# The low part of every fourth weight block made by an accumulating DMA instead of VectorE

## The chip, the cores and the metric

The kernel runs on one core of a Trainium2 chip. The metric is the device time of one execution, in microseconds. The core has five engines with instruction streams of their own: TensorE (PE in the profile, with its weight loads as PEld), VectorE (DVE), ScalarE (ACT), GpSimd (POOL) and SyncE (SP). Sixteen DMA engines move data; a transfer is issued from the stream of SP, ACT or POOL.

## The reference

Two transformer blocks run one after the other on 256 tokens of width 2048, all in float32. The first block has softmax attention with ALiBi (8 heads), a retention layer (4 heads), gates, and a gated feed-forward layer of inner width 5632. The second has gated linear attention, differential attention, and a feed-forward layer with a short convolution, again of inner width 5632. Cut to what matters here, the work is a chain of dense products with weights that are each used once:

```python
proj = h @ w_in                       # 2048 x 13312, first block
merged = sigmoid(ga) * (oa @ w_o_attn) + sigmoid(gr) * (orr @ w_o_ret)
x = x + merged @ w_out
g, u = split(rms_norm(x, g_ffn) @ w_ffn_in)       # 2048 x 11264
x = x + (silu(g) * u) @ w_ffn_out                 # 5632 x 2048
...                                   # second block, of the same kind
```

The weights come to some 500 MB in float32.

## The kernel before

Each matrix product in float32 is made of three products of reduced operands. A weight block `w` is split into a high part (`hi`, `w` rounded to the format fp32r) and a low part (`lo = w - hi`); the activations are split in the same way. TensorE then adds `x_hi*hi`, `x_lo*hi` and `x_hi*lo` in one accumulator (lines 1170 to 1172, and lines 1208 and 1210 for the products with the weights as the stationary operand).

The weights are cut into 946 blocks of 128 x 1024 float32 (512 KB). The class `Sched` streams them in one fixed order. Three of its methods matter here:

- `load` (line 79) issues the DMA of a block into a tile `wraw` from SP's stream. There are 4 such tiles (`RAW_BUFS`), so the load of block n+4 waits until everything that reads the tile of block n is done.
- `split` makes `hi` by a ScalarE copy (line 100, tile `whi`) and `lo` by a VectorE subtraction (line 101, tile `wlo`). There are 4 tiles of each (`PART_BUFS`), so the split of block n waits until TensorE has finished with block n-4. A few blocks of two tasks, whose numbers are in the set `roomy`, get a tile `wparts` of another pool.
- `take` is called ahead of the products of each block. It asks for loads up to 6 blocks ahead and for splits up to 3 blocks ahead (2 for the first 16 blocks), and hands out the parts of the next block.

The norms of line 356 on POOL divide the program into four stages: the first block's mixer (288 weight blocks), its feed-forward layer (264), the second block's mixer (130) and its feed-forward layer (264).

The rest of the work (attention, retention, gated linear attention, norms, evacuations of accumulators) is written as generators, which `tick` advances by a step after each block; so it stands between the blocks in each engine's stream. Every engine works through its stream in order. SP's stream holds little but the loads. POOL's stream holds 49 tensor operations and 10 loads of other inputs.

For a block that is used as the moving operand, TensorE runs 12 products of 512 columns: for two groups of 128 tokens and two groups of 128 inputs, one with `hi` and the high part of x, one with `hi` and the low part, one with `lo`.

Of the kernel before, what the change touches and what calls it, by code (L numbers as in the profile page):

```python
# [14 lines left out]
AF = mybir.ActivationFunctionType  # L15
ALU = mybir.AluOpType
# [28 lines left out]
class Sched:  # L45
# [39 lines left out]
    def split(self, upto):  # L85
        nc = self.nc
        if self.hold is not None:
            upto = min(upto, self.hold)
        while self.n_split <= min(upto, len(self.blocks) - 1):
            self.load(self.n_split)  # L90
            n = self.blocks[self.n_split].shape[1]
            raw = self.raw.pop(self.n_split)
            if self.n_split in self.roomy:
                both = self.room([P, 2, 1024], F32R, name="wparts")
                hi, lo = both[:, 0], both[:, 1]
            else:
                hi = self.wp.tile([P, 1024], F32R, name="whi", tag="whi", bufs=PART_BUFS)
                lo = self.wp.tile([P, 1024], F32R, name="wlo", tag="wlo", bufs=PART_BUFS)
            for c in self.cuts(self.n_split, n):
                nc.scalar.activation(hi[:, c], raw[:, c], AF.Copy)  # L100
                nc.vector.tensor_tensor(lo[:, c], raw[:, c], hi[:, c].bitcast(F32), op=ALU.subtract)  # L101
                if self.n_split == 0:
                    self.between()
            self.parts[self.n_split] = (hi, lo)
            self.n_split += 1
# [79 lines left out]
def body(ctx, tc, A, out):  # L185
# [62 lines left out]
    def halves(dst, src, scale=None):  # L248
        split(dst[:, 0], dst[:, 1], src, scale)
# [154 lines left out]
    def turned(key, f0, srcs, use=None, then=None, gain=None, wait=2):  # L404

        def part(j):
            def fn():
                m = mtile()
                turn(m, srcs, j)
                f = f0 + 2 * j  # L410
                if use is not None:
                    use(f, m)
                    return
                h_tile(key, f)
                dst = st[key][f // 4][:, f % 4:f % 4 + 2]
                if gain is None:
                    split(dst[:, :, 0], dst[:, :, 1], pairs(m))
                else:
                    highs_lows([(dst[:, i], m[:, cols(i, S)], gain(f + i)) for i in range(2)])
            return fn  # L420
        for j in range(2):
            step_of(key, f0 + 2 * j, part(j), wait + j)
            if then is not None:
                step_of(key, f0 + 2 * j, lambda f=f0 + 2 * j: then(f), wait + j + 1)
# [610 lines left out]
    def act_split(f):  # L1035
        h_tile("act", f)
        dst = st["act"][f // 4][:, f % 4:f % 4 + 2]
        split(dst[:, :, 0], dst[:, :, 1], pairs(st.pop(("cv", f))))
# [313 lines left out]
```

## Time and profile before

| what | value |
|---|---|
| median of 2 runs | 2761.0 us (2760.97 to 2761.03) |
| the profiled execution's own time | 2761.08 us |
| its span, first to last instruction | 2759.3 us |
| TensorE busy | 99% of the span |
| VectorE busy | 54% |
| ScalarE busy | 47% |
| GpSimd busy | 2% |
| the 16 DMA engines busy, SP's queue | 53.3% |
| granted TensorE clock, mean | 0.999 of full speed |

A row of a group of instructions reads: line, engine, operation, the tile written and the tiles read, shapes, count; then the busy time and the mean duration in nanoseconds; then the idle time of that engine just before them, and what ended it. A row of a timeline reads: start and duration in microseconds, engine, line, operation, tiles, count, and in brackets the idle time before it and what ended that.

### The profile page before, as it was taken

What the parts mean: (1) busy time and instruction counts of PE and PEld (TensorE: products, weight loads), DVE (VectorE), ACT (ScalarE), POOL (GpSimd) and SP (SyncE); (2) the same over time, 40 slices, a digit from 0 to 9 for tenths busy, and PEclk for the clock granted to TensorE, in tenths of its full rate; (3) what the DMA queues carried; (4) which work ended last, traced back from release to release, by engine and by line L of the source; (5) the groups of instructions that cost most, each with busy time, mean ns of one, the idle gap of its engine ahead of it and who ended that gap; (6) DMA issues with size and microseconds to landing.
All of it is one profiled execution on the core that took longest, in us unless ns stands there. A gap on an engine that the chain in (4) does not pass through costs nothing.

```text
span 2759.3 us, 33343 instructions
## 1 busy us (share of the span) xinstructions
PE 2728.7 (99%) x12876; PEld 2274.1 (82%) x12876; DVE 1502.6 (54%) x1732; ACT 1299.0 (47%) x1673; POOL 61.6 (2%) x63
## 2 busy tenths in 40 slices
PE   8999999999999999999999999999989999999998
PEld 6888788888888888888888888888878888888887
DVE  4456555554455554545455547775555554455555
ACT  5445444444444444334444454554455554445543
POOL 0000000000000000000000001110000000000000
PEclk9999999999999999999999999999999999999999
DMA  7554446555555555555555555445545555555554
GB/s 255 178 180 167 160 168 217 195 187 194 191 185 189 190 191 184 192 196 191 191 185 189 189 202 174 145 145 191 183 169 185 189 182 192 194 187 183 187 190 151
DMA packets 141936, 511.41 MB, mean 185 GB/s; under 512 B 16912, under 2 KB 17296, under 8 KB 141008
## 3 DMA queue, kind: packets, MB, share of 16 engines
q1 hardware_dynamic: 140256, 500.62, 53.3%
q0 software_dynamic: 1376, 8.65, 0.9%
q8 instruction: 101, 1.65, 0.2%
q14 instruction: 59, 0.48, 0.0%
q10 hardware_dynamic: 144, 0.01, 0.0%
HBM read 507.11 MB, written 2.10 MB: 185 GB/s over the span
## 4 chain that ended last, share of the span: by engine, by line
PE 97%; DVE 1%; ACT 1%; issue 0%; DMA 0%; SPq 0%; POOLq 0%; DVEq 0%; POOL 0%; ACTq 0%
PE acc L1172 27%; PE acc L1170 27%; PE acc L1171 27%; PE acc L1208 8%; PE acc L1210 4%; PE m L402 2%; PE m L797 1%; DMA wraw<-in_w_va 0%; DVE hx L239 0%; DVE wlo L101 0%; PE m L520 0%; PE m L599 0%; PE m L452 0%; DVE x L239 0%; ACT junk L336 0%
## 5 line engine op out<-in xcount | busy, mean ns | idle before, releaser
L101 DVE TENSOR_TENSOR wlo<-wraw,whi 128x1024 fp32r<-128x1024 f32 (+1 forms) x934 | 1144.4, 1226 | 1003.9 <-ACT whi L100 999.1
L100 ACT ACTIVATE whi<-wraw 128x1024 fp32r<-128x1024 f32 (+1 forms) x934 | 986.7, 1058 | 944.5 <-PE acc L1171 896.0
L1170 PE MATMUL acc<-whi,hx 128*128 128x512 f32 x2160 | 858.1, 397 | 11.3 <-ACT hx L230 5.9
L1172 PE MATMUL acc<-wlo,hx 128*128 128x512 f32 x2160 | 844.1, 391 | 0.5 <-DVE wlo L101 0.5
L1171 PE MATMUL acc<-whi,hx 128*128 128x512 f32 x2160 | 842.6, 390 | 0.0
L1170 PEld LDWEIGHTS acc<-whi,hx 128*128 128x128 f32 x2160 | 406.4, 188 | 94.7 <-ACT whi L100 6.3
L1172 PEld LDWEIGHTS acc<-wlo,hx 128*128 128x128 f32 x2160 | 406.1, 188 | 88.0 <-DVE wlo L101 1.7
L1171 PEld LDWEIGHTS acc<-whi,hx 128*128 128x128 f32 x2160 | 406.8, 188 | 83.6 <-issue 1.9
L1208 PE MATMUL acc<-hx,whi 128*128 128x512 f32 x912 | 330.6, 404 | 0.0
L1170 PE MATMUL acc<-whi,act 128*128 128x512 f32 (+1 forms) x704 | 271.0, 385 | 0.0
L1172 PE MATMUL acc<-wlo,act 128*128 128x512 f32 (+1 forms) x704 | 269.8, 383 | 0.0
L1171 PE MATMUL acc<-whi,act 128*128 128x512 f32 (+1 forms) x704 | 269.8, 383 | 0.0
L1210 PE MATMUL acc<-hx,wlo 128*128 128x256 f32 x912 | 255.7, 280 | 0.0
L1208 PEld LDWEIGHTS acc<-hx,whi 128*128 128x128 f32 x912 | 171.3, 188 | 38.9 <-issue 0.5
L1210 PEld LDWEIGHTS acc<-hx,wlo 128*128 128x128 f32 x912 | 172.4, 189 | 1.0 <-issue 0.5
L1172 PEld LDWEIGHTS acc<-wlo,act 128*128 128x128 f32 x704 | 132.3, 188 | 26.3
L1170 PEld LDWEIGHTS acc<-whi,act 128*128 128x128 f32 x704 | 132.4, 188 | 25.5
L1171 PEld LDWEIGHTS acc<-whi,act 128*128 128x128 f32 x704 | 132.4, 188 | 25.4
L228 ACT ACTIVATE t<-acc 128x256 f32<-128x256 f32 x57 | 21.9, 383 | 96.7 <-PE acc L1210 96.6
L239 DVE SCALAR_TENSOR_TENSOR cv<-m,c_conv_w,cv 128x255 f32<-128x255 f32 x88 | 40.4, 480 | 24.0 <-ACT cv L1018 22.5
L1170 PE MATMUL acc<-whi,mg 128*128 128x512 f32 x128 | 50.7, 396 | 0.0
L1172 PE MATMUL acc<-wlo,mg 128*128 128x512 f32 x128 | 49.9, 390 | 0.0
(279 smaller groups left out, 1825.4 us busy)
## 6 DMA issues: line engine op xcount, KB each, us to landing
wraw<-in_w_f SPq DMA_DIRECT2D x352, 512.0 KB, 3.4
wraw<-in_w_f1o SPq DMA_DIRECT2D x88, 512.0 KB, 4.3
wraw<-in_w_f2o SPq DMA_DIRECT2D x78, 512.0 KB, 3.3
wraw<-in_w_ga SPq DMA_DIRECT2D x34, 512.0 KB, 3.4
wraw<-in_w_vr SPq DMA_DIRECT2D x32, 512.0 KB, 3.3
wraw<-in_w_gr SPq DMA_DIRECT2D x32, 512.0 KB, 3.2
wraw<-in_w_gret SPq DMA_DIRECT2D x32, 512.0 KB, 3.3
wraw<-in_w_or SPq DMA_DIRECT2D x32, 512.0 KB, 3.4
```

The source lines that it names most:

```text
L100: nc.scalar.activation(hi[:, c], raw[:, c], AF.Copy)
L101: nc.vector.tensor_tensor(lo[:, c], raw[:, c], hi[:, c].bitcast(F32), op=ALU.subtract)
L228: nc.scalar.activation(out, in_, AF.Copy)
L239: nc.vector.scalar_tensor_tensor(out, a, s, b, op0=op0, op1=op1)
L402: nc.tensor.transpose(m[:, (i * len(srcs) + k) * P:][:, :P], src[:, (n * j + i) * P:][:, :P], ident)
L797: nc.tensor.matmul(m[:, ks], prev[1][:, ks], prev[0][:, ks], start=True, stop=True)
L1170: nc.tensor.matmul(accs[k], x[:, 0], hi[:, w], start=b, stop=False)
L1171: nc.tensor.matmul(accs[k], x[:, 1], hi[:, w], start=False, stop=False)
L1172: nc.tensor.matmul(accs[k], x[:, 0], lo[:, w], start=False, stop=e)
L1208: nc.tensor.matmul(acc, hi[:, w], x.rearrange("p a b -> p (a b)"), start=(k == first), stop=False, skip_group_check=True)
L1210: nc.tensor.matmul(acc[:, S:], lo[:, w], x[:, 0], start=False, stop=(k == last), skip_group_check=True)
```

## The change

For every block whose number has the remainder 3 by 4, from block 11 on and outside `roomy`, the low part is made in another way. ScalarE writes the high part as before, and then the same rounding with the sign turned over into `lo`, so `lo = -hi`. A DMA issued from POOL's stream then adds the raw block onto it: `lo = -hi + w`. VectorE's subtraction is left out for these blocks. Nothing else differs, and the numbers of tiles stay as they were. The program holds 231 such blocks: in POOL's stream 71 of these DMAs stand ahead of the norm that closes the first stage, 66 more ahead of the second, 31 ahead of the third, and 63 after that.

```diff
+            if self.n_split % 4 == 3 and self.n_split > 8 and self.n_split not in self.roomy:
+
+                nc.scalar.activation(hi[:, :n], raw[:, :n], AF.Copy)
+                nc.scalar.activation(lo[:, :n], raw[:, :n], AF.Copy, scale=-1.0)
+                nc.gpsimd.dma_start(lo[:, :n], raw[:, :n], accum_op=ALU.add)
+                self.parts[self.n_split] = (hi, lo)
+                self.n_split += 1
+                continue
             for c in self.cuts(self.n_split, n):
                 nc.scalar.activation(hi[:, c], raw[:, c], AF.Copy)
                 nc.vector.tensor_tensor(lo[:, c], raw[:, c], hi[:, c].bitcast(F32), op=ALU.subtract)
```

ScalarE's stream in the first feed-forward layer. Before, around the split of the activations (`act`), the copies of the high parts stand alone:

```order
335 L228 ACTIVATE act<-m 128x2x256
336 L100 ACTIVATE whi<-wraw 128x1024 x6
337 L637 ACTIVATE gate<-acc,r_x_97 128x512 x2
338 L100 ACTIVATE whi<-wraw 128x1024 x9
339 L228 ACTIVATE act<-m 128x2x256
```

With the change, the same place (the lines of the program are 8 further on):

```order
620 L108 ACTIVATE whi<-wraw 128x1024 x2
621 L101 ACTIVATE whi<-wraw 128x1024
622 L102 ACTIVATE wlo<-wraw 128x1024
623 L108 ACTIVATE whi<-wraw 128x1024 x3
624 L645 ACTIVATE gate<-acc,r_x_97 128x512 x2
```

After every three copies (line 108) there are two for one block (lines 101 and 102), the second into `wlo`.

SP's stream with what each load waits for, where the loads of the first feed-forward layer's output weights begin. Before, every load waits for VectorE, which is the subtraction that read the tile last:

```order
401 L79 DMA wraw<-in_w_f 128x1024 [waits DMAHW0_49,DVE_49]
402 L79 DMA wraw<-in_w_f1o 128x1024 [waits DMAHW1_49,DVE_49]
403 L79 DMA wraw<-in_w_f1o 128x1024 [waits DMAHW2_49,DVE_49]
404 L79 DMA wraw<-in_w_f1o 128x1024 [waits DMAHW3_49,DVE_49]
405 L79 DMA wraw<-in_w_f1o 128x1024 [waits DMAHW4_49,DVE_49]
406 L79 DMA wraw<-in_w_f1o 128x1024 [waits DMAHW5_49,DVE_49]
```

With the change:

```order
401 L79 DMA wraw<-in_w_f 128x1024 [waits DMAHW1_49,DVE_49]
402 L79 DMA wraw<-in_w_f1o 128x1024 [waits DMAHW0_49,DMASW1_49]
403 L79 DMA wraw<-in_w_f1o 128x1024 [waits DMAHW2_49,DVE_49]
404 L79 DMA wraw<-in_w_f1o 128x1024 [waits DMAHW3_49,DVE_49]
405 L79 DMA wraw<-in_w_f1o 128x1024 [waits DMAHW5_49,DVE_49]
406 L79 DMA wraw<-in_w_f1o 128x1024 [waits DMAHW4_49,DMASW2_49]
```

Every fourth load now waits for a DMA of POOL's queue (the semaphores DMASW) in place of VectorE, and the loads behind it in SP's stream come after it.

POOL's stream around the attention of the second block, with the change:

```order
167 L103 DMA wlo<-wraw 128x1024 [waits DMASW0_49,DMAHW4_49,PE_49,Activation_49]
168 L789 TENSOR_TENSOR Kl<-E,gqk 128x256 [waits DVE_49]
169 L789 TENSOR_TENSOR Kl<-E,gqk 128x256 x2
170 L103 DMA wlo<-wraw 128x1024 [waits DMASW2_49,DMASW1_49,DMAHW0_49,PE_49,Activation_49]
171 L789 TENSOR_TENSOR Kl<-E,gqk 128x256 [waits DVE_49]
```

Before, the operations of line 789 (then 781) stood there with no DMA between them. Now the accumulating DMAs (line 103), which wait for ScalarE, stand in the same stream.

## Rows read from the trace of the kernel before

**Rows 1.** The page: busy time of each engine; the chain of waits.
```profile
PE 2728.7 (99%) x12876; PEld 2274.1 (82%) x12876; DVE 1502.6 (54%) x1732; ACT 1299.0 (47%) x1673; POOL 61.6 (2%) x63
PE 97%; DVE 1%; ACT 1%; issue 0%; DMA 0%; SPq 0%; POOLq 0%; DVEq 0%; POOL 0%; ACTq 0%
```

**Rows 2.** The waits of TensorE: waited for, us in total, times, longest.
```profile
PE acc L1172 <- DVE wlo L101: 0.5, 1, 0.5
...
PEld acc L1172 <- DVE wlo L101: 1.7, 3, 0.9
```

**Rows 3.** The page's groups: the two halves of the split.
```profile
L101 DVE TENSOR_TENSOR wlo<-wraw,whi 128x1024 fp32r<-128x1024 f32 (+1 forms) x934 | 1144.4, 1226 | 1003.9 <-ACT whi L100 999.1
L100 ACT ACTIVATE whi<-wraw 128x1024 fp32r<-128x1024 f32 (+1 forms) x934 | 986.7, 1058 | 944.5 <-PE acc L1171 896.0
```

**Rows 4.** Timeline of ScalarE, first feed-forward layer.
```profile
1000.04 1.06 ACT L100 ACTIVATE whi<-wraw 128x1024 fp32r<-128x1024 f32 x1 [1.66 <-PE acc L1171]
1002.76 1.06 ACT L100 ACTIVATE whi<-wraw 128x1024 fp32r<-128x1024 f32 x1 [1.66 <-PE acc L1171]
1005.48 1.06 ACT L100 ACTIVATE whi<-wraw 128x1024 fp32r<-128x1024 f32 x1 [1.66 <-PE acc L1171]
1008.20 1.06 ACT L100 ACTIVATE whi<-wraw 128x1024 fp32r<-128x1024 f32 x1 [1.66 <-PE acc L1171]
1009.79 0.69 ACT L637 ACTIVATE gate<-acc,r_x 128x512 f32<-128x512 f32 x1 [0.53 <-PE acc L1172]
```

**Rows 5.** Timeline of all engines, the same stretch: VectorE and SP.
```profile
1001.13 1.23 DVE L101 TENSOR_TENSOR wlo<-wraw,whi 128x1024 fp32r<-128x1024 f32 x1 [1.49 <-ACT whi L100]
...
1002.39 13.93 SPq L79 DMA_DIRECT2D wraw<-in_w_f  x6
```

**Rows 6.** The tile wraw: time from issue to landing of its 947 loads.
```profile
DMA to landing us min/median/max: 3.0/3.6/11.0
```

**Rows 7.** DMA issues from POOL: count, KB each, median us from issue to landing.
```profile
xr<-in_x_rows POOLq DMA_DIRECT2D x2, 1024.0 KB, 8.9
x<-in_x_rows POOLq DMA_DIRECT2D x2, 1024.0 KB, 8.4
post<-in_attn_post_norm POOLq DMA_DIRECT2D x1, 1024.0 KB, 6.8
post<-in_ffn_post_norm POOLq DMA_DIRECT2D x1, 1024.0 KB, 8.5
decay<-in_decay POOLq DMA_DIRECT2D x1, 768.0 KB, 6.8
e<-in_mk POOLq DMA_DIRECT2D x1, 512.0 KB, 9.1
```

**Rows 8.** Timeline of POOL: the norms that close the four stages, one issue.
```profile
860.18 1.62 POOL L356 TENSOR_TENSOR r_x<-ms,neghalf 128x2 f32<-128x2 f32 x1 [402.45 <-DVE ms L355]
1592.86 1.61 POOL L356 TENSOR_TENSOR r_x<-ms,neghalf 128x2 f32<-128x2 f32 x1 [731.06 <-DVE ms L355]
...
1895.26 0.62 POOL L955 DMA_DIRECT2D post<-in_attn_post_norm  x1
2025.80 1.64 POOL L356 TENSOR_TENSOR r_x<-ms,neghalf 128x2 f32<-128x2 f32 x1 [24.72 <-DVE ms L355]
2745.06 0.66 POOL L356 TENSOR_TENSOR r_f<-ms,neghalf 128x1 f32<-128x1 f32 x1 [716.47 <-DVE ms L355]
```

**Rows 9.** Windows: engines' busy time, granted clock, DMA share, GB/s.
```profile
860.00:1593.00 733.00, 733.00 (x3291) 606.69 (x3290) 371.83 (x344) 317.05 (x341) 1.76 (x2) 1.00 0.56 190
...
2005.00:2010.00 5.00, 4.21 (x15) 3.05 (x15) 4.06 (x7) 2.79 (x9) 0.00 (x0) 0.71 0.46 144
```

**Rows 10.** Timeline of TensorE around the turn of the second block.
```profile
1999.73 0.39 PE L1172 MATMUL acc<-wlo,hx 128*128 128x512 f32 x1
2003.42 0.63 PE L402 MATMUL m<-c_ident,x 128*128 128x128 f32 x4 [3.31 <-DVE x L239]
...
2017.61 0.66 PE L402 MATMUL m<-c_ident,x 128*128 128x128 f32 x4 [1.66 <-DVE x L239]
2018.02 0.48 PE L1170 MATMUL acc<-whi,hx 128*128 128x512 f32 x1
```

## The prediction

> **What bounds the kernel now.** I read the busy times and the chain of waits first. TensorE is busy for 99% of the span and makes up 97% of the chain [rows 1]; the reader is to see that nothing but its stream of products sets the end. Then its waits: for the low parts that VectorE makes it waits 0.5 + 1.7 = 2.2 us in the whole run [rows 2]. So taking work from VectorE can give back about 2 us at most. The question is only whether the new way of making the low part is late.
>
> For that I read how early a block is ready, in a stretch of pure weight products. ScalarE starts a copy at 1000.04, 1002.76, 1005.48 and 1008.20 us, each time let go by TensorE's last use of a high part [rows 4]. So a block takes 2.72 us, four take 10.88 us, and a split starts as soon as the parts of four blocks earlier are free. Since three other blocks come in between, the low part has 3 x 2.72 us, and two products of its own block (0.45 us), before it is missed: 8.6 us. Now it takes 1.06 us on ScalarE, and VectorE ends at 1001.13 + 1.23 = 1002.36, which is 2.3 us after the start [rows 4, 5]. SP's next load is issued at 1002.39, at once after it [rows 5]: the raw tile is what that load waited for. A load lands 3.6 us after its issue in the median, 3.0 at least [rows 6]. From the start of a split to the landing of the load that takes over its raw tile is thus 2.3 + 3.6 = 5.9 us, and 10.88 us are there: 5.0 us to spare.
>
> **What the change removes.** 231 subtractions of 1.23 us, 283 us of VectorE [rows 3]. They lie beside TensorE's work, so this is worth at most the 2.2 us above; I take nothing.
>
> **What it adds on ScalarE.** 231 second copies of 1.06 us, 245 us [rows 3]. ScalarE is idle for 1.66 us ahead of each copy [rows 4], so the second fits and leaves 0.6 us. An evacuation of 0.69 us [rows 4] that falls right there is late by some tenths, and the accumulators have spare tiles; I take nothing, with 0.1 us as an upper end in the round trip below, which is inside its uncertainty. In POOL's stream the Kl operations of the second mixer now stand behind a DMA that waits for ScalarE. Their results are used a step of the generator, one block, later: nothing from below, 31 DMAs x 2.2 us = 68 us from above. I take nothing, since that stage also has the longest time for a block.
>
> **What it adds in DMA time: two round trips.** Call D the time from ScalarE's second copy to the landing of the accumulating DMA. After the copies (2 x 1.06 us and two handovers, 2.2 us) come D and then the use. The first round trip is that of the part tiles: D may be 8.6 - 2.3 = 6.3 us before TensorE waits. The second is that of the raw tiles, and it is tighter: every fourth load now waits for the accumulating DMA, and four blocks later its block is split. One turn takes 2.3 + D + 3.6 us. It fits in 10.9 us up to D = 5.0 us. Above that TensorE waits for the rest once in four blocks, and the turn itself is then the pace.
>
> D has no row, since nothing accumulates before. From below: a plain load of 512 KB from SP lands after 3.0 us at the fastest [rows 6]. From above: the slowest POOL load, 512 KB behind two others, takes 9.1 us [rows 7]. The transfer reads 512 KB of raw block and 512 KB of negated high part, so each DMA engine takes in as much as for a plain 1 MB; the nearest rows are the loads of 1 MB from POOL that had the queue to themselves, 6.8 and 8.5 us [rows 7]. I take the lower, 6.8 us, because here the weight loads partly wait for this DMA instead of running beside it, and nothing of it comes from outside the core's own memory. POOL's stream is held for 0.6 us by an issue [rows 8], which is inside the 6.8.
>
> Against this stands a rule. These rows say 6.8 us or more for 1 MB. The Trainium skill, "DMA: Bandwidth & Descriptors", section "Anatomy of one DMA — SWDGE (gpsimd) path", fits a transfer issued from GpSimd by 2.0 us plus the bytes over 436 GB/s; an estimate from that page is 3.2 us for 512 KB and 4.4 us for 1 MB. By it the turn is 2.3 + 4.4 + 3.6 = 10.3 us and the sum is nothing; by the row it is the sum below. The row has the weight loads beside it, as here (in such a stage the engines are busy 56% of the time [rows 9]), so I go by the row. The skill's "Collectives: The Full Stack", on why a reduce-scatter moves half of what an all-gather does, says that an add in a DMA takes two source reads on one ring, which is the doubling used here; no run before shows it.
>
> **The sum.** The turn is 2.3 + 6.8 + 3.6 = 12.7 us. What four blocks take differs by stage, because other products lie between them. The norms that close the stages start at 860.2, 1592.9, 2025.8 and 2745.1 us [rows 8]. With 288, 264, 130 and 264 blocks, four blocks take 11.9, 11.1, 13.3 and 10.9 us. The stages hold 71, 66, 31 and 63 of the new DMAs, so the waits are 71 x 0.8 = 57, 66 x 1.6 = 106, 0, and 63 x 1.8 = 113 us: 276 us in all. The profiled execution took 2761.1 us (span 2759.3, and 1.8 around it), the same as the median of the runs to 0.1 us. The forecast is **3037 us**.
>
> With the upper end, D = 9.1, the turn is 15.0 us and the waits are 71 x 3.1, 66 x 3.9, 31 x 1.7 and 63 x 4.1: 788 us, so 3549 us. Such pauses may also cost clock. In this trace TensorE stood still for 3.3 us until 2003.42, and from 2005 to 2010 the granted clock was 0.71, part of it at the lower of its two levels, 1.2 in place of 2.4 GHz [rows 9, 10]; that is 0.29 x 5 = 1.5 us lost. A pause of 1.66 us [rows 10] was followed by products 0.23 us apart, no loss. In the forecast the pauses are below 1.9 us, so nothing is added; at the upper end 129 pauses of 3.9 us and more could add 129 x 1.5 = 190 us, 3740 us. With the lower end, D = 3.0, nothing waits: 2761 us.
>
> **Rivals.** A measurement of this kernel tells 2% (55 us) from no change. By the sum that is a turn of 11.4 us: D = 5.5 us.
>
> - *The DMA is in time* (not slower): D stays below 5.5 us, because its two reads come out of memory on the core and the 5.0 us to spare are covered by an idle queue. For it speaks that SP's load of 512 KB takes 3.6 us under the same traffic [rows 6], and the fit above; against it that no POOL load landed in under 6.8 us [rows 7]. Place: the raw round trip in the two feed-forward stages. Time 2761 to 2816 us. Chance 0.28.
> - *The add itself is slow*: the engines pass the sums at less than the rate of a copy, or the descriptors for two reads take longer to write than for one. With D = 12 the turn is 17.9 us, the waits 71 x 6.0, 66 x 6.8, 31 x 4.6 and 63 x 7.0, 1459 us: 4220 us, and more with the clock. No row speaks for or against it, since no add in a DMA is in the trace. From D = 9.1 it decides. Chance 0.20.
> - *Faster by over 2%*: VectorE's 283 us would have to be on the path, and 2.2 us are [rows 2]. Chance 0.02.
>
> My forecast, D from 5.5 to 9.1 us, has the rest, 0.50; its own range is 2816 to 3740 us. For 8 in 10 the range takes in the case in time and leaves out the slow add: 2755 to 3740 us. Faster 0.02, within 2% 0.28, slower 0.50 + 0.20 = 0.70.
>
> **What would show it.** In the changed profile the 231 DMAs from POOL should land 6.8 us after issue in the median; below 5.0 the first rival holds, above 9.1 the second. TensorE should wait in every fourth block, once in 12.7 us in the first feed-forward layer, with ScalarE's copies held by a load of wraw (a DMA as the releaser, where now it is TensorE), or the third product of a block held by the new DMA. In the second block's mixer there should be almost no wait. VectorE's busy time should fall by 283 us and ScalarE's rise by 245 us. The prediction is wrong in its mechanism if TensorE waits while the raw tiles are full, for instance behind ScalarE's or POOL's stream, and in its size if D is not 6.8 us.

## The result and the profile after

| | before | changed |
|---|---|---|
| median of the runs | 2761.0 us | 2782.3 us (2780.2 and 2784.4) |
| ratio, 95% interval | | 1.0077 [1.006, 1.0093] |
| repeated on another chip | 2761.7 us | 2783.0 us, 1.0077 [1.0062, 1.0092] |
| span of the profiled execution | 2759.3 us | 2782.6 us |

The change costs 21 us, 0.8%. The forecast was a loss of 276 us. Of the cases told ahead, the first rival happened: the DMA is in time.

The page of the changed kernel, busy times, the two DMA queues that matter (packets, MB, share of 16 engines) and the chain by engine:

```profile
PE 2739.2 (98%) x12876; PEld 2276.8 (82%) x12876; DVE 1228.9 (44%) x1501; ACT 1512.6 (54%) x1904; POOL 254.3 (9%) x294
...
q1 hardware_dynamic: 140256, 500.62, 50.4%
q0 software_dynamic: 34640, 129.78, 25.0%
...
PE 92%; DMA 4%; DVE 2%; ACT 2%; issue 1%; SPq 0%; POOL 0%; POOLq 0%; DVEq 0%; ACTq 0%
```

Against [rows 1], VectorE is 273.7 us less busy and ScalarE 213.6 us more, both near the 283 and 245 us of the sum. POOL's queue q0 rises from 0.9% to 25.0% of the engines. That is 695.7 - 24.8 = 671 us, or 2.9 us of every engine for each of the 231 adds. TensorE itself is 10.5 us longer busy, more than half of it clock, as shown below.

The view of the tile `wlo`, time from issue to landing of the adding DMAs:

```profile
DMA to landing us min/median/max: 4.5/4.7/6.4
```

And of the tile `wraw`, its loads:

```profile
DMA to landing us min/median/max: 3.0/4.3/10.8
```

The row that the forecast rested on said 6.8 us [rows 7]; the add takes 4.7. The loads land later than before, 4.3 against 3.6 us [rows 6]. One turn in the first feed-forward layer shows how it stands to the use (timeline of ScalarE, POOL and SP):

```profile
1005.63 1.06 ACT L101 ACTIVATE whi<-wraw 128x1024 fp32r<-128x1024 f32 x1 [1.71 <-PE acc L1179]
1006.59 1.04 ACT L102 ACTIVATE wlo<-wraw 128x1024 fp32r<-128x1024 f32 x1
...
1007.93 0.86 POOL L103 DMA_DIRECT2D wlo<-wraw  x1 [10.71 <-ACT wlo L102]
...
1012.68 0.33 SPq L79 DMA_DIRECT2D wraw<-in_w_f  x1
```

The copies end 2.0 us after the start, POOL issues 0.3 us later, and SP's load, which waited for the landing, follows 4.75 us after the issue. That is 7.05 us, where TensorE misses the low part after 8.6: 1.5 us to spare. The load of 1012.68 lands after 3.6 us, at 1016.28, and the next split through that tile is due 10.9 us after 1005.63, at 1016.5: that round trip fits as well, just. (In this turn the split starts only at 1017.27, behind an evacuation on ScalarE.)

What runs beside the add is seen in the DMA view of its transfer, 1009.36 to 1012.32 us:

```profile
q0 software_dynamic: 144, 0.52, 99.5%
q1 hardware_dynamic: 18, 0.07, 7.4%
```

The weight queue q1, which holds the engines half of the time on average, moves 0.07 MB here, and it holds the engines for at most 9% of the time during each add between 900 and 1100 us. By then the other raw tiles are full, and SP's stream stands at the load that waits for this very add.

The loss begins with single late blocks. TensorE's waits, first of the matmuls (waited for, us, times, longest):

```profile
PE acc L1180 <- DMA wlo<-wraw: 9.8, 10, 1.8
...
PE m L751 <- DMA lmr<-in_w_alpha_up: 3.2, 1, 3.2
...
PE acc L1218 <- DMA wlo<-wraw: 0.8, 2, 0.4
```

And of the weight loads, which run ahead of the matmuls:

```profile
PEld acc L1180 <- DMA wlo<-wraw: 15.3, 16, 2.2
...
PEld acc L1218 <- DMA wlo<-wraw: 1.4, 2, 0.7
```

Only 18 of 231 blocks are late. Of these 18, 15 begin right behind another instruction of ScalarE (of all 231, 90 do), and 9 have an add that lands after 5.3 us or more (of all 231, 32 do): a late start and a late landing use up the 1.5 us. The matmuls stand still for 10.6 us for them and for 3.2 us for one load of the second block's attention (`lmr`), and TensorE is 10.5 us longer busy: 24.3 us, against 23.3 us of span. POOL's stream shows the second wait and the stages:

```profile
865.83 1.62 POOL L364 TENSOR_TENSOR r_x<-ms,neghalf 128x2 f32<-128x2 f32 x1 [0.83 <-DVE ms L363]
1603.05 1.63 POOL L364 TENSOR_TENSOR r_x<-ms,neghalf 128x2 f32<-128x2 f32 x1 [0.83 <-DVE ms L363]
1645.80 0.89 POOL L737 DMA_DIRECT2D lmr<-in_lm  x1
1646.34 0.90 POOL L739 DMA_DIRECT2D lmr<-in_w_alpha_up  x1
...
2045.43 0.70 POOL L364 TENSOR_TENSOR r_x<-ms,neghalf 128x2 f32<-128x2 f32 x1 [24.68 <-DVE ms L363]
...
2768.29 0.67 POOL L364 TENSOR_TENSOR r_f<-ms,neghalf 128x1 f32<-128x1 f32 x1 [18.58 <-DVE ms L363]
```

With [rows 8], the stages are longer by 5.7, 4.5, 9.4 and 3.6 us. The third, where the sum had no loss, has the most. Its loads came from POOL right after the norm before; now they are issued 42.8 us after it, behind four adds that wait for their blocks.

The clock: windows of TensorE's busy time behind the longest wait for an add (1291.12), around the wait for `lmr` (1654.05), and at the end of the second block's mixer; the third number from the end is the granted clock.

```profile
1286.00:1291.00 5.00, 3.33 (x15) 2.44 (x13) 2.44 (x2) 2.09 (x2) 0.00 (x0) 1.00 0.91 210
1291.00:1296.00 5.00, 4.88 (x14) 3.87 (x15) 0.01 (x1) 0.88 (x1) 0.00 (x0) 0.66 0.79 286
...
1654.00:1662.00 8.00, 7.95 (x23) 5.71 (x24) 1.96 (x3) 3.96 (x7) 0.00 (x0) 0.62 0.56 205
2018.00:2038.00 20.00, 13.78 (x56) 10.43 (x55) 13.63 (x28) 11.38 (x31) 0.57 (x1) 0.83 0.45 158
```

After a pause of 1.8 us the clock was 0.66 for 5 us, part of it at 1.2 GHz: 0.34 x 5 = 1.7 us more. After 3.2 us it was 0.62 for 8 us, 3.0 us more. At the end of the mixer it was 0.83 for 20 us, 3.4 us, where the kernel before had 0.91, 1.8 us; e2, a run without any add, has 0.83 there too, so these 1.6 us are not shown to come from the adds. That is 6.3 of the 10.5 us; the rest is not located.

### The profile page after: what moved, and what is told of

The parts are those of the page before. It is cut to its first block, busy times and chain, and to the rows that moved or that the text cites. A ratio compares the mean times of both kernels' runs of the same rounds, so it can differ in the third digit from the quotient of the medians.

```text
span 2782.6 us, 33776 instructions
## 1 busy us (share of the span) xinstructions
PE 2739.2 (98%) x12876; PEld 2276.8 (82%) x12876; DVE 1228.9 (44%) x1501; ACT 1512.6 (54%) x1904; POOL 254.3 (9%) x294
## 4 chain that ended last, share of the span: by engine, by line
PE 92%; DMA 4%; DVE 2%; ACT 2%; issue 1%; SPq 0%; POOL 0%; POOLq 0%; DVEq 0%; ACTq 0%
PE acc L1180 26%; PE acc L1178 26%; PE acc L1179 26%; PE acc L1216 7%; PE acc L1218 3%; DMA wlo<-wraw 3%; PE m L410 2%; PE m L805 0%; DMA wraw<-in_w_va 0%; ACT wlo L102 0%; DVE wlo L109 0%; ACT whi L108 0%; DVE hx L247 0%; DMA lmr<-in_w_alpha_up 0%; DMA wraw<-in_w_out 0%
## 5 line engine op out<-in xcount | busy, mean ns | idle before, releaser
L109 DVE TENSOR_TENSOR wlo<-wraw,whi 128x1024 fp32r<-128x1024 f32 (+1 forms) x703 | 862.7, 1228 | 1203.3 <-ACT whi L108 1200.8
L108 ACT ACTIVATE whi<-wraw 128x1024 fp32r<-128x1024 f32 (+1 forms) x703 | 742.7, 1057 | 556.3 <-PE acc L1179 523.3
L103 POOL DMA_DIRECT2D wlo<-wraw x231 | 199.8, 865 | 2305.2 <-ACT wlo L102 1867.6
L101 ACT ACTIVATE whi<-wraw 128x1024 fp32r<-128x1024 f32 x231 | 244.4, 1058 | 251.7 <-PE acc L1179 230.9
L102 ACT ACTIVATE wlo<-wraw 128x1024 fp32r<-128x1024 f32 x231 | 241.6, 1046 | 0.0
```

Of the source, the lines that this page charges most:

```text
L101: nc.scalar.activation(hi[:, :n], raw[:, :n], AF.Copy)
L102: nc.scalar.activation(lo[:, :n], raw[:, :n], AF.Copy, scale=-1.0)
L103: nc.gpsimd.dma_start(lo[:, :n], raw[:, :n], accum_op=ALU.add)
```

## The experiments

Ratios are to the kernel before, run on the same chip, with 95% intervals.

**e1: a plain copy.**

```diff
-                nc.gpsimd.dma_start(lo[:, :n], raw[:, :n], accum_op=ALU.add)
+                nc.gpsimd.dma_start(lo[:, :n].bitcast(F32), raw[:, :n])
```

> The accumulating DMA is made a plain copy of the raw block onto the low part, so the low part of these 231 blocks holds the weight itself; times are read, not values. Theory A (the price of the DMA is 2.0 us plus the rows of one engine, 8 x 0.34 us, and the loss of 21 us comes from the few blocks that it makes late): a row falls from 340 ns to about 160, the landing from 4.7 to about 3.4 us, the waits of TensorE for it from 16.7 us to under 3; time 2763 to 2770 us. Theory B (the second copy on ScalarE delays the splits): still 2780 us. Theory C (the sum is right and only the price of D was too high): as A, since D falls by 1.4 us.

2772.7 us, 1.0039 [1.0024, 1.0054]: half of the loss goes. The landing of the copies:

```profile
DMA to landing us min/median/max: 2.8/2.9/5.5
```

POOL's queue on its page:

```profile
q0 software_dynamic: 34640, 129.78, 11.6%
```

A copy holds each engine for 1.3 us (11.6% of 2770.4 us, less 24.8, by 231), an add for 2.9. The add costs the engines 2.2 times a copy, and these 1.6 us are nearly all of the 1.8 us between landings of 2.9 and 4.7. So the doubling that the forecast took was right. The time is 3 us above what was expected. Two blocks were still late (4.5 us in the matmuls), and their delay began ahead of the transfer:

```profile
1278.01 1.05 ACT L102 ACTIVATE wlo<-wraw 128x1024 fp32r<-128x1024 f32 x1
1281.94 0.54 POOL L103 DMA_DIRECT2D wlo<-wraw  x1 [13.69 <-PE acc L1180]
```

POOL issues 2.9 us after the copy's end instead of 0.3, in both cases, and then the two copies land late as well, after 4.4 and 5.5 us. More on this at the end.

**e2: the second copy without the DMA.**

```diff
-                nc.gpsimd.dma_start(lo[:, :n], raw[:, :n], accum_op=ALU.add)
+                nc.vector.tensor_tensor(lo[:, :n], raw[:, :n], hi[:, :n].bitcast(F32), op=ALU.subtract)
```

> The second ScalarE copy stays, VectorE's subtraction comes back behind it, no DMA. Theory A: the copy lies in idle time, 2761 to 2764 us. Theory B: 2775 us or more.

2765.1 us, 1.0011 [1.0001, 1.0021]. ScalarE's extra work of some 214 us costs about 3 us, a little over the expected bound. It is not the loss. How it costs them is not shown: in the profiles TensorE's waits grow by 1 us and its busy time by 3.0 us.

**e3: the three loads of the second attention earlier in the program.**

```diff
+    def gla_loads():
+        st["lmr"] = lmr = slot([P, 16, P], name="lmr")
+        nc.gpsimd.dma_start(lmr[:, :12], A["lm"])
...
+    C(gla_loads)
     alloc("dv", [P, 2, 1024])
...
-        nc.gpsimd.dma_start(lmr[:, :12], A["lm"])
```

> The three POOL loads for the second block's gated attention are put into the program at the start of that stage, ahead of the accumulating DMAs they stood behind. Theory A: the wait of 3.2 us for one of them and the half clock after it (6.8 us at half) go, so 5 to 8 us less than the changed kernel, about 2775 us. If POOL's order costs nothing elsewhere, no other wait changes. Rival: the loss is in the late blocks alone, no difference beyond 2 us.

2778.8 us, 1.0061 [1.0046, 1.0076]. The wait for `lmr` is gone from the profile; the waits for the adds are as before (9.6 us in the matmuls). The medians differ by 4 us from the changed kernel, less than expected, and the intervals overlap; the row, not the time, is what shows it.

**e4: the add twice in a row.** It tests the prediction's sum with a longer D.

```diff
-                nc.scalar.activation(lo[:, :n], raw[:, :n], AF.Copy, scale=-1.0)
-                nc.gpsimd.dma_start(lo[:, :n], raw[:, :n], accum_op=ALU.add)
+                nc.scalar.activation(lo[:, :n], raw[:, :n], AF.Copy, scale=-2.0)
+                nc.gpsimd.dma_start(lo[:, :n], raw[:, :n], accum_op=ALU.add)
+                nc.gpsimd.dma_start(lo[:, :n], raw[:, :n], accum_op=ALU.add)
```

> The negated copy is taken twice as large and the raw block is added twice by two DMAs, the second waiting for the first, so the low part of these blocks is doubled. D becomes 2 x 4.7 + 0.4 = 9.8 us. By the prediction's sum with this D, a turn of 2.0 + 9.8 + 3.6 = 15.4 us and waits of 71 x 3.5, 66 x 4.3, 31 x 2.1 and 63 x 4.5 us: 881 us more than before, 3640 us, and up to 190 us more if the pauses halve the clock. A rival (part tiles alone set the limit, loads do not): a turn of 2.0 + 9.8 + 2.3 = 14.1 us, 540 us more, 3300 us.

4194 us, 1.519 [1.516, 1.522]. The busy times of its page:

```profile
PE 3169.4 (76%) x12876; PEld 2533.1 (60%) x12876; DVE 1234.1 (29%) x1501; ACT 1515.0 (36%) x1904; POOL 445.4 (11%) x525
```

The waits of its matmuls for the adds:

```profile
PE acc L1181 <- DMA wlo<-wraw: 866.1, 200, 8.9
PE acc L1219 <- DMA wlo<-wraw: 98.9, 25, 7.0
```

965 us of waits, where the sum with its new D gave 881. That the two are near is luck, because D was not 9.8 us. The first of the two adds lands after 4.7 us in the median, the second later:

```profile
DMA to landing us min/median/max: 4.5/5.9/8.0
```

With two handovers of 0.3 us D was about 11.2 us, and with this D the sum gives a turn of 16.8 us and 1204 us. The kernel is in fact 1432 us longer: beside the waits TensorE is 440.7 us longer busy with the same products, since the mean granted clock fell to 0.878, far over the 190 us put as the bound of the clock. Nor were ScalarE's copies for these blocks let go by a load, as the sum has it, but by TensorE:

```profile
L101 ACT ACTIVATE whi<-wraw 128x1024 fp32r<-128x1024 f32 x231 | 244.1, 1057 | 1075.0 <-PE acc L1180 1054.1
```

The two adds of one block also show what company does, with the same source and the same size. The queues during the first (1539.53 to 1544.30 us, landing after 4.7 us):

```profile
q0 software_dynamic: 144, 0.52, 62.1%
q1 hardware_dynamic: 46, 0.19, 11.2%
```

And during the second (1544.55 to 1551.23 us, landing after 6.6 us):

```profile
q0 software_dynamic: 144, 0.52, 39.6%
q1 hardware_dynamic: 212, 0.74, 38.3%
```

One of the pauses:

```profile
1525.71 0.39 PE L1180 MATMUL acc<-whi,hx 128*128 128x512 f32 x1
1531.98 0.79 PE L1181 MATMUL acc<-wlo,hx 128*128 128x512 f32 x1 [5.88 <-DMA wlo<-wraw]
1532.57 0.63 PE L1179 MATMUL acc<-whi,hx 128*128 128x512 f32 x1
1533.00 0.63 PE L1180 MATMUL acc<-whi,hx 128*128 128x512 f32 x1
```

Ahead of a pause, products stand 0.23 us apart; these stand 0.43.

**e5: every second block.**

```diff
-            if self.n_split % 4 == 3 and self.n_split > 8 and self.n_split not in self.roomy:
+            if self.n_split % 2 == 1 and self.n_split > 8 and self.n_split not in self.roomy:
```

> Every second block takes the new way (odd numbers from 9), about 460 DMAs. Theory A' (D is short only because the engines' weight queue is nearly empty while a DMA adds): four blocks now hold 4 loads of 1.27 us and two adds of 8 x 0.34 = 2.7 us per engine, 10.5 of 10.9 us, so loads and adds meet, D goes from 4.7 to 6 or more, and the turn of 2.3 + 6.2 + 4.0 = 12.5 us costs 1.4 to 1.6 us per four blocks in the feed-forward layers: 2950 to 3150 us. Rival (an add takes 4.7 us whatever runs beside it): twice the loss of the changed kernel, about 2805 us.

3042.6 us, 1.102 [1.095, 1.108], as the theory of the empty queue had it. The two queues on its page:

```profile
q1 hardware_dynamic: 140256, 500.62, 46.6%
q0 software_dynamic: 67904, 250.90, 45.3%
```

The landing of its adds:

```profile
DMA to landing us min/median/max: 4.5/6.1/13.5
```

With the engines 92% taken, loads and adds meet, and the same add takes 6.1 us. Here ScalarE's copies do wait for loads as well, 70.1 us for the blocks of `in_w_f` alone.

**e6: the add reads HBM.**

```diff
-                nc.gpsimd.dma_start(lo[:, :n], raw[:, :n], accum_op=ALU.add)
+                nc.gpsimd.dma_start(lo[:, :n], self.blocks[self.n_split], accum_op=ALU.add)
```

> The DMA adds the block from HBM once more in place of the raw tile, so the raw tile is free after ScalarE's second copy and the next load runs beside the add. The tight round trip is gone, that of the part tiles (D up to 6.3 us) is left. Theory A': with weight loads beside it D is 6 to 7.5 us and TensorE waits 0 to 1.2 us in every fourth block of the feed-forward layers: 2770 to 2920 us. Rival (D stays at 4.7 us): the waits vanish, 2763 to 2772 us.

3152.9 us, 1.141 [1.138, 1.144], well above the expected 2920. The landing of the adds:

```profile
DMA to landing us min/median/max: 5.2/7.9/9.2
```

The queues while one is moving (1116.8 to 1122.0 us):

```profile
q0 software_dynamic: 140, 0.51, 62.4%
q1 hardware_dynamic: 163, 0.59, 32.1%
```

The raw tile is free early, so loads run beside the add, and it lands after 7.9 us. That is within the prices of the POOL loads in [rows 7], 6.8 to 9.1 us, which read HBM beside weight loads too. The longest of TensorE's wait groups, of 271 us in all:

```profile
PE acc L1180 <- DMA wlo<-in_w_f: 113.8, 72, 3.5
```

The run changes two things at once, the source and the company; e5 and the two adds of e4 change the company alone.

**e7 and e8: a fifth raw tile.** e7, the control, has the first of these two edits, e8 both.

```diff
-        return tmp.tile([P, 512], F32, name=name, tag="w", bufs=6)
+        return tmp.tile([P, 512], F32, name=name, tag="w", bufs=4)
...
-RAW_BUFS = 4
+RAW_BUFS = 5
```

> Control for the next run: the changed kernel with 4 in place of 6 tiles of 512 columns for small work. Theory: no more than 5 us off the changed kernel, 2780 to 2788 us.

> The control with a fifth raw tile. The load that waited for the adding DMA now waits for the subtraction of the block before, so loads run beside the add. Theory A': the landing of the add rises from 4.7 us to 5.2 to 5.8, the weight queue's share of the engines during it from 3% to over 20%, and since only the round trip of the part tiles is left the time is 2765 to 2785 us. Rival: the landing stays at 4.7 us and TensorE no longer waits for it, 2765 us.

2781.1 us, 1.0073 [1.0058, 1.0088], and 2781.3 us, 1.0068 [1.0051, 1.0085]. The fifth tile changes nothing. Both forecasts of e8 fail: the landing stays at 4.7 us and the waits stay too. SP's waits in e8:

```profile
SPq L79 <- DMA wlo<-wraw: 636.8, 230, 10.6
```

Those of the weight loads on TensorE:

```profile
PEld acc L1180 <- DMA wlo<-wraw: 14.9, 18, 2.2
```

With five tiles the ring is full a block later, but still full: the loads wait for 230 of the 231 adds as with four. So the empty queue remains (the weight queue holds the engines for at most 12% of the time during each add between 900 and 1100 us); and the raw tiles are not the limit that the late blocks break.

**e9: the blocks with remainder 1.**

```diff
-            if self.n_split % 4 == 3 and self.n_split > 8 and self.n_split not in self.roomy:
+            if self.n_split % 4 == 1 and self.n_split > 8 and self.n_split not in self.roomy:
```

> The blocks with remainder 1 by 4 take the new way in place of remainder 3. Theory (a block is late when its split starts late behind the two evacuations on ScalarE that end a task of 8 blocks, and a slow handover or landing comes on top): the splits of these blocks stand elsewhere by two blocks, so the start is late less often, the waits fall from 15 to under 8 us and the time to 2768 to 2777 us. Rival (the late landings alone): no difference beyond 3 us.

2779.2 us, 1.0062 [1.0047, 1.0077], beside 2783.0 us, 1.0077 [1.0062, 1.0092], for the changed kernel on the same chip. TensorE's weight loads still wait 12.3 us for the adds, not under 8. Inconclusive: the place behind the evacuations is at most a part of it.

> The changed kernel once more, on the chip of the next three runs. 2780 to 2784 us, TensorE's waits for the adding DMAs 14 to 17 us.

The waits there were 14.6 us in the weight loads, inside the expected range.

**e10 and e11: a fifth pair of part tiles,** e11 with the early loads of e3.

```diff
-LEAD_SPLIT = 3
+LEAD_SPLIT = 4
...
-PART_BUFS = 4
+PART_BUFS = 5
...
-        return tmp.tile([P, S], F32, name=name, tag="u", bufs=6)
+        return tmp.tile([P, S], F32, name=name, tag="u", bufs=5)
...
-        return tmp.tile([P, 384], F32, name=name, tag="v", bufs=5)
+        return tmp.tile([P, 384], F32, name=name, tag="v", bufs=3)
...
-        return tmp.tile([P, 512], F32, name=name, tag="w", bufs=6)
+        return tmp.tile([P, 512], F32, name=name, tag="w", bufs=4)
```

> Five pairs of part tiles in place of four and splits asked for 4 blocks ahead (with fewer tiles for small work: 4, 3 and 5 in place of 6, 5 and 6). Theory (the limit that late blocks break is the round trip of the part tiles): it grows by 2.7 us to 11.3 us, the slowest add takes 10.3 us from the start of its split, so TensorE's waits for the adding DMAs vanish and 2764 to 2772 us are left, with the late load of the second block's attention. Rival (the raw tiles set the limit): no change, 2780 us.

> The same with the three POOL loads put at the start of their stage. Theory: neither wait is left, 2760 to 2766 us, no faster than the kernel before by more than 2 us, since VectorE's work is not on the path.

2768.0 us, 1.0023 [1.0013, 1.0032], and 2766.7 us, 1.0018 [1.0009, 1.0028]. What is left of TensorE's waits for the adds in e10:

```profile
PEld acc L1218 <- DMA wlo<-wraw: 2.3, 1, 2.3
...
PEld acc L1180 <- DMA wlo<-wraw: 0.5, 1, 0.5
```

Against the repeated run, 15 of the 21 us are gone with the fifth pair. So the late blocks are late in the round trip of the part tiles, as expected. Three things blur the size: the wait for `lmr` is gone from e10 as well, though its loads were not moved, so e11 had little left to win; the splits are also asked for a block earlier; and the cut of the small-work tiles, with which the fifth pair fits into the memory, was run alone only in part (e7). Even with both cures the change stays 5 us behind the kernel before; e2 shows some 3 of them as ScalarE's copy. No run was faster than the kernel before.

## Why the prediction was wrong

- **What bounds the kernel** held. VectorE lost 274 us of work and nothing came back.
- **The second copy on ScalarE**, priced at nothing, costs about 3 us (e2), little beside the 276 us of the sum.
- **D is the step that failed:** "I take the lower, 6.8 us". D is 4.7 us from issue to landing, 5.0 with the handover, just on the edge that the prediction itself had worked out. The doubling was right (2.9 against 1.3 us of each engine). What was wrong was the company in the row: 1 MB from HBM beside weight loads. The prediction even said that the weight loads would partly wait for this DMA instead of running beside it, and used that only to pick the lower of two crowded rows. With company the same add takes 5.9 us (the second one in e4) or 6.1 (e5), and from HBM 7.9 (e6), so company explains over 1 us of the error and the source in HBM may hold the rest, which no run shows by itself; in the changed kernel the weight queue moved 0.07 MB during a transfer of 0.52.
- **The rule** set against the row, the fit of the Trainium skill, "DMA: Bandwidth & Descriptors", section "Anatomy of one DMA — SWDGE (gpsimd) path", gave as an estimate 4.4 us for the doubled bytes and 3.2 for a copy. The traces have 4.7 and 2.9: it was nearer than the row where the engines were free. Where they were not it was too low, by 1.7 us in e5 and 3.5 in e6.
- **The sum** was right in kind: with D about 5.0 us it gives no waits, and with a D well above that nearly every block of the new kind is waited for (225 of 231 in e4). Its size is not confirmed. With e4's measured D of 11.2 us it gives 1204 us, and e4 is 1432 us longer; the sum has no term for the clock.
- **Which round trip is tighter** was wrong for this kernel: the raw tiles were put first. The load behind an add meets an empty queue too (3.6 us in the turn shown), so the loop just closes; a fifth raw tile changed nothing (e8), a fifth part pair took 15 of the 21 us away (e10). In e4 too TensorE released last: in the turn of 1537.24 us the block's remaining products, at the lower clock, took 3.9 us from the landing and the load 3.5, so the two trips lie close together.
- **POOL's order**, priced at nothing with an upper end of 68 us, costs 3.2 us and some 3.0 us of clock behind it. It was looked for in the Kl products and came in three loads that had been early only because POOL's stream was empty.
- **The clock** was left out below pauses of 1.9 us. One of 1.8 us already cost 1.7 us, and in e4 the clock took 441 us, over twice the bound.

## What to carry to other kernels

A transfer's price depends on what shares the engines at that moment. When the change itself holds back the other stream, as here a load that waits for the DMA's source tile, price it by an idle queue first, and treat the crowded row as the upper end. A match of two sums proves little until each term is read: 881 against 965 us in e4 came from a D that was too small and a clock that was left out. Where the sum ends on the edge of a budget (5.0 against 5.0 us), forecast "no change with a few late cases" and count what can be late. Before moving work onto an idle engine's stream, list what in that stream was early only because nothing stood ahead of it.

## What was not expected of the hardware

- An add of 512 KB in the core's memory by a DMA from POOL lands after 4.7 us, a copy after 2.9; POOL's issue takes 0.86 instead of 0.53 us.
- At eight of POOL's 231 issues, the same eight in the repeated run, the issue follows ScalarE's copy after 0.8 to 1.6 us instead of 0.3. At the late block of 1291.12 us in the changed kernel it was 1.6 us, and the add then landed after 6.2 us (columns as in the timelines above):

```profile
1281.34 1.05 ACT L101 ACTIVATE whi<-wraw 128x1024 fp32r<-128x1024 f32 x1
1282.29 1.05 ACT L102 ACTIVATE wlo<-wraw 128x1024 fp32r<-128x1024 f32 x1
...
1284.93 0.86 POOL L103 DMA_DIRECT2D wlo<-wraw  x1 [12.06 <-ACT whi L108]
...
1291.12 0.50 PE L1180 MATMUL acc<-wlo,hx 128*128 128x512 f32 x1 [1.79 <-DMA wlo<-wraw]
```

In e1, which has four such issues, the DMA at the same place of the program came 2.9 us after the copy. No run changed POOL's instructions alone, so what it is stays open.

- A pause of 1.79 us was followed by a lower clock (above), one of 1.63 us before 2517.73 us was not; in the kernel before, 1.66 us was not [rows 10].
